# Spacing x's k-tiles 2176 instead of 2048 bytes apart in SBUF, in a one-core hybrid encoder layer

## The chip, the cores and the metric

The kernel runs on one core of one Trainium2 chip. The metric is the device time of one execution in microseconds (us). Three runs of the kernel before gave 1111.41, 1112.29 and 1112.52 us, so the time before is 1112.29 us.

The engines are named as in the profile: PE (TensorE, matmuls), PEld (TensorE loading the stationary operand), DVE (VectorE), ACT (ScalarE), POOL (GpSimd) and SP (which issues DMAs). SBUF is the on-chip memory with 128 partitions; an address below is the number of bytes from the start of a partition. PSUM is where matmuls accumulate.

## The reference

One encoder layer over 256 tokens of width 2048, all in float32:

```python
hn = _rmsnorm(h, norm_w[i])
proj = hn @ w_in[i]                       # 2048 -> 9 x 2048
q, v, f_fwd, f_bwd, z_a, b_gate, c_gate, h_b, z_b = jnp.split(proj, IN_SPLITS, axis=-1)
o_a = _hgrn2_bidirectional(jax.nn.silu(q), v, f_fwd, f_bwd, lb_all[:, i])
o_a = _head_rmsnorm(o_a, hgrn_norm_w[i]) * jax.nn.silu(z_a)
y_b = b_gate * _short_conv(c_gate * h_b, conv_w[i])
o_b = _rmsnorm(y_b, conv_norm_w[i]) * jax.nn.silu(z_b)
h = h + jnp.concatenate([o_a, o_b], axis=-1) @ w_out[i]      # 4096 -> 2048
gate = jax.nn.sigmoid(h @ w_ple_gate[i])                     # 2048 -> 2048
h = h + (p[i] @ w_ple[i]) * gate
return _rmsnorm(h, final_norm_w)
```

Most of the arithmetic is the product of x with w_in.

## The kernel before

**Splitting.** A float32 matrix is held as two parts, a rounded high part and the rest as a low part, and a product is made of three: high by high, high by low, low by high. Weights come from HBM in tiles of 1 MB into `raw` buffers (three of them in turn). ACT writes the high part into an `spl` buffer (L121), DVE the low part (L122). There are five `spl` buffers of 8192 bytes per partition, in turn. x is split once at the start into `xs` (L367 and L368), which stays until the last projection has ended.

**xs.** It has 16 k-tiles, one for each 128 rows of x transposed. A k-tile holds the high part (256 tokens, 1024 bytes) and behind it the low part (1024 bytes).

**The projections.** `gemm_part` makes, for each k-tile and each half m of 256 output columns, two matmuls: L427 with the weights' high part stationary and the whole k-tile (512 columns) moving, and L425 with the weights' low part stationary and x's high part alone (256 columns) moving. So a k-tile has two pairs of L427 and L425. There are 56 such projections: three at the start that advance together, and 53 of 16 k-tiles each. In some projections the order of the four matmuls is turned in k-tiles 1 and 3, or 9 and 11 (`TURNED`, `LATER`). The first value and gate projections (`gemm_two`, L446 to L448) and the later ones (`half` and `three`, L547 to L549) have x stationary and 512 columns of weights moving. All of these read xs. The output product (`pa`, `pb`), the gate (`pg<-spl,ht`) and the per-layer embedding (`pp<-spl,pt`), L547 to L549 and L1026 to L1028, do not.

**Order.** A scheduler sets each engine's order by priorities; only the first three projections are written out by hand. The weights are fetched ahead of their use through SP's queue.

**Small buffers.** `wz` is a block of zeros for 13 matmuls that run ahead of the first weights (L266). `early` is a buffer of 8192 bytes with the scans' mask in columns 0 to 255, later one of the norms (`rbc2`) in 256 to 511, the triangular masks in 512 to 1023, and two zeroed score buffers (`scm`) from 1024 and 1536; POOL fills it at the start (L277 to L290). `mx`, `et` and `esum` serve the lower bounds of the forget gates, once. `rw` holds the tokens' norms spread over 128 columns, for two matmuls once (L402).

**Places.** The allocator's addresses, in bytes, with the place modulo 1024:

| buffer | address | modulo 1024 |
|---|---|---|
| spl, five | 54208, and 8192 more each | 960 |
| xs, k-tile k | 95168 + 2048 k | 960 |
| ht0, after xs | 111552 | 960 |
| mixb, mixa (concatenated branches) | 147392, 196544 | 960 |
| pt (embedding input, split) | 172000 | 992 |
| s (scores, tag "s") | 187840 | 448 |
| early | 18304 | 896 |

Within an spl buffer the parts lie 1024 bytes apart, and the second half of 128 output columns 512 bytes behind the first. So a stationary operand begins at 960 or at 448 modulo 1024.

Of the kernel before, what the change touches and what calls it, by code (L numbers as in the profile page):

```python
# [8 lines left out]
F32 = mybir.dt.float32  # L9
F32R = mybir.dt.float32r  # L10
# [7 lines left out]
P = 128  # L18
D = 2048
T = 256  # L20
NKT = D // P
# [116 lines left out]
def tile_hymba_encoder(  # L138
# [15 lines left out]
    act, dve, pool, pe = nc.scalar, nc.vector, nc.gpsimd, nc.tensor  # L154
    out2 = out[0].rearrange("(m p) d -> p m d", p=P)

    const = ctx.enter_context(tc.tile_pool(name="const", bufs=1))
# [3 lines left out]
    xsp = xsctx.enter_context(tc.tile_pool(name="xsp", bufs=1))  # L161
# [3 lines left out]
    xp = xctx.enter_context(tc.tile_pool(name="xp", bufs=1, side="left"))  # L165
# [43 lines left out]
    for u in range(2):  # L209
        for half in range(2):  # L210
            oblocks.append([])
            for q in ORDER:
                k = 16 * half + 2 * q
# [21 lines left out]
    rx, rb, rf, most, dummy = (few[:, 2 * j : 2 * j + 2] for j in range(5))  # L235
# [21 lines left out]
    cvw, th = vec[:, 3:6, :], vec[:, 6:10, :].rearrange("p (d j) c -> p d j c", d=2)  # L257


    wz = const.tile([P, P], F32, name="wz")  # L260
    dve.memset(wz, 0.0)

    act.activation(dummy[:, 0:1], wz[:, 0:1], AF.Copy)
# [6 lines left out]
    ident = const.tile([P, P], F32, name="ident")  # L270
# [1 line left out]
    ones = const.tile([P, 1], F32, name="ones")  # L272
    pool.memset(ones, 1.0)

    early = const.tile([P, 2048], F32, name="early")
    smask = early[:, 0:T]
    pool.memset(smask, 1.0)  # L277
    pool.memset(smask.rearrange("p (c t) -> p c t", t=CH)[:, :, 0:1], 0.0)
# [16 lines left out]
        dve.memset(t, 0.0)  # L295


    mx = const.tile([P, 2, 16], F32, name="mx")
    et = const.tile([P, 2, 2, 16], F32, name="et")
    esum = const.tile([P, 2, 16], F32, name="esum")  # L300
    lb = const.tile([P, 2, 16], F32, name="lb")
    oml = const.tile([P, 2, 16], F32, name="oml")
    noml = const.tile([P, 2, 16], F32, name="noml")
# [57 lines left out]

    xs = xsp.tile([P, NKT, 2, T], F32R, name="xs")

    def x_split(kt):
        act.activation(xs[:, kt, 0, :], xf32[:, kt, :], AF.Copy, scale=nw[:, kt : kt + 1])  # L367
# [5 lines left out]
    rbc = const.tile([P, T], F32, name="rbc")  # L373
    rbc2 = early[:, T : 2 * T]
    ss8 = const.tile([P, 2, 4], F32, name="ss8")
    rw = [const.tile([P, P], F32, name=f"rw{m}") for m in range(2)]

    def load_tokens(m):
        nc.sync.dma_start(xf32[:, 8 * m : 8 * m + 8].rearrange("p k t -> p (k t)"), xtok[:, m])
# [12 lines left out]
    def x_norms():  # L392
        dve.tensor_reduce(out=rx, in_=ss8, op=ALU.add, axis=AX.X)
        act.activation(rx, rx, AF.Sqrt, bias=epst, scale=1.0 / D)
        dve.reciprocal(out=rx, in_=rx)
        for m in range(2):
            dve.tensor_copy(rw[m], rx[:, m : m + 1].broadcast_to([P, P]))

    def norms_spread():
        rps = psm.tile([P, 512], F32, tag="y", name="rps")  # L400
        for m in range(2):
            pe.matmul(rps[:, m * P : (m + 1) * P], lhsT=rw[m], rhs=ident, start=True, stop=True)  # L402
        dve.tensor_copy(rbc, rps[:, :T])  # L403
        dve.tensor_tensor(out=rbc2, in0=rbc, in1=rbc, op=ALU.mult)

# [114 lines left out]
    ap_ = actx.enter_context(tc.tile_pool(name="ap", bufs=1, side="right"))  # L520
    for m in range(2):
        at(2 + m, lambda m=m: load_tokens(m))
    for c in range(4):
        at(6 + c, lambda c=c: x_squares(c))
    at(11, x_norms)
    at(14, norms_spread)


# [395 lines left out]
    for i in range(8):  # L924
# [50 lines left out]
        for src, z, n in ((mixa, i - 1, len(SUMS)), (mixb, i - SUMS[0], len(sumb32))):  # L975
            if 0 <= z < n:
                k = 2 * SUMS[z]
# [3 lines left out]
                else:  # L981
                    t = ctmp.tile([P, 4, P], F32, tag="hb", name=f"sb{i}", bufs=2)
# [80 lines left out]
    for u in range(2):  # L1063
# [9 lines left out]
        for src, sums, main, other, scale in ((mixa, suma, psg, psm, False), (mixb, sumb, psm, psg, True)):  # L1073
            name = f"p{'ab'[scale]}{u}"
            acc = four(main, name)
            parts = oblocks[2 * u + scale]
            if u == 0 and not scale:
                for z in range(len(SUMS)):
                    k = 2 * SUMS[z]
# [186 lines left out]
```

## Time and profile before

| | |
|---|---|
| median of three runs | 1112.29 us (1111.41 to 1112.52) |
| the profiled execution | 1112.2 us, of which the span from first to last instruction is 1110.5 us |
| granted TensorE clock | 0.998 |
| PE busy | 1100.5 us, 99% |
| PEld busy | 945.7 us, 85% |
| DVE busy | 851.4 us, 77% |
| ACT busy | 677.3 us, 61% |
| POOL busy | 269.1 us, 24% |

A line of a group has the source line, the engine, the operation, output and inputs by the program's names, the shapes and the count; then the busy time in us and the mean duration of one in ns; then the engine's idle time ahead of them. Matmuls overlap, so their durations add up to more than the time that they take; a row of the timeline begins with the start in us, and the distance from one start to the next says how long a matmul holds the engine. A line of the form `L783 ... x16: 723/748/769, 90.8 to 501.3` has the least, median and greatest duration in ns, then the first and last start in us.

### The profile page before, as it was taken

To read this page: it belongs to the slowest core of one execution; us is meant where nothing else is said; L and a number is where in the kernel's file an instruction comes from. 1 tells how busy PE (TensorE), PEld (TensorE's weight loads), DVE (VectorE), ACT (ScalarE), POOL (GpSimd) and SP (SyncE) were. 2 spreads that over 40 slices of the span, in tenths; PEclk is the share of its full clock that TensorE was granted. 3 is DMA by queue.
4 is the path that set the end of the run, shared out by engine and by line. 5 is a ranking of instruction groups with operands and counts; after the bars stand their busy time and mean duration, and the time that the engine had idled before them with its cause. 6 is when DMAs were issued, how large, how long until landed. Compare 5 with 4: busy or idle time off the path is not lost.

```text
span 1110.5 us, 16882 instructions
## 1 busy us (share of the span) xinstructions
PE 1100.5 (99%) x6455; PEld 945.7 (85%) x6455; DVE 851.4 (77%) x1127; ACT 677.3 (61%) x946; POOL 269.1 (24%) x215
## 2 busy tenths in 40 slices
PE   9999999999999999999999999999999999999997
PEld 8888888888888888888888888888888888888886
DVE  7799578896889778997657758856667888887673
ACT  6786577667876697575545535535546575575562
POOL 1045015203530325043334223424331000000101
PEclk9999999999999999999999999999999999999999
DMA  9755454564457744758999998999979887887542
GB/s 340 272 187 190 153 190 157 171 242 153 161 162 258 292 152 152 231 172 228 298 310 250 270 334 231 282 345 254 288 196 306 318 299 286 286 312 253 193 133 76
DMA packets 69808, 260.44 MB, mean 235 GB/s; under 512 B 7008, under 2 KB 16608, under 8 KB 52192
## 3 DMA queue, kind: packets, MB, share of 16 engines
q1 hardware_dynamic: 60480, 242.25, 62.1%
q0 software_dynamic: 8960, 16.78, 10.0%
q8 instruction: 51, 0.84, 0.3%
q10 hardware_dynamic: 288, 0.34, 0.1%
q14 instruction: 29, 0.24, 0.1%
HBM read 257.25 MB, written 35.65 MB: 264 GB/s over the span
## 4 chain that ended last, share of the span: by engine, by line
PE 98%; DMA 1%; ACT 0%; SPq 0%; DVE 0%; DVEq 0%; issue 0%; ACTq 0%
PE a L427 37%; PE a L425 19%; PE avz L547 3%; PE avz L548 3%; PE avz L549 3%; PE pg L1027 3%; PE pg L1026 3%; PE pg L1028 3%; PE pa L547 2%; PE pa L548 2%; PE pa L549 2%; PE a L446 1%; PE a L448 1%; PE a L447 1%; PE pb_sc L548 1%; PE pb_sc L549 1%
## 5 line engine op out<-in xcount | busy, mean ns | idle before, releaser
L122 DVE TENSOR_TENSOR spl<-raw,spl 128x1024 fp32r<-128x1024 f32 (+2 forms) x419 | 505.0, 1219 | 163.6 <-ACT spl L121 160.2
L427 PE MATMUL a<-xs,spl 128*128 128x512 f32 x1792 | 617.3, 395 | 0.6 <-ACT spl L121 0.6
L121 ACT CAST spl<-raw 128x1024 fp32r<-128x1024 f32 (+2 forms) x419 | 414.1, 999 | 255.0 <-PE a L425 81.9
L425 PE MATMUL a<-xs,spl 128*128 128x256 f32 x1792 | 483.8, 278 | 0.0
L427 PEld LDWEIGHTS a<-xs,spl 128*128 128x128 f32 x1792 | 332.2, 188 | 73.6 <-ACT spl L121 1.0
L425 PEld LDWEIGHTS a<-xs,spl 128*128 128x128 f32 x1792 | 334.6, 188 | 5.8 <-DVE spl L122 0.5
L1143 POOL TENSOR_TENSOR hh<-hh,fw 128x512 f32<-128x512 f32 (+1 forms) x9 | 11.0, 1227 | 250.7 <-ACT gt L1142 248.0
L487 ACT COPY r<-a 128x256 f32<-128x256 f32 x112 | 40.5, 368 | 37.3 <-PE a L425 35.8
L547 PE MATMUL avz<-spl,xs 128*128 128x512 f32 x138 | 54.0, 391 | 0.0
L549 PE MATMUL avz<-spl,xs 128*128 128x512 f32 x138 | 53.7, 389 | 0.0
L548 PE MATMUL avz<-spl,xs 128*128 128x512 f32 x138 | 53.7, 389 | 0.0
L1026 PE MATMUL pg<-spl,ht 128*128 128x512 f32 (+1 forms) x120 | 45.2, 377 | 0.0
L1027 PE MATMUL pg<-spl,ht 128*128 128x512 f32 (+1 forms) x120 | 45.1, 376 | 0.0
L1028 PE MATMUL pg<-spl,ht 128*128 128x512 f32 (+1 forms) x120 | 45.0, 375 | 0.0
L716 POOL TENSOR_TENSOR qc<-pf,ge 128x256 f32<-128x256 f32 x16 | 18.3, 1148 | 105.8 <-ACT dd L706 91.8
L492 POOL TENSOR_TENSOR xf<-xf,rbc 128x1024 f32<-128x1024 f32 x8 | 19.9, 2486 | 94.0 <-DVE rbc L403 50.2
L121 ACT CAST spl<-early 128x1024 fp32r<-128x1024 f32 (+1 forms) x29 | 28.7, 990 | 19.1 <-PE pb_y L549 7.5
L122 DVE TENSOR_TENSOR spl<-early,spl 128x1024 fp32r<-128x1024 f32 (+1 forms) x29 | 32.9, 1147 | 9.2 <-ACT spl L121 8.8
L547 PE MATMUL pa<-spl,mixa 128*128 128x512 f32 x88 | 34.5, 392 | 0.0
L549 PE MATMUL pa<-spl,mixa 128*128 128x512 f32 x88 | 34.3, 389 | 0.0
L548 PE MATMUL pa<-spl,mixa 128*128 128x512 f32 x88 | 34.2, 389 | 0.0
L716 POOL TENSOR_TENSOR kc<-dd,ge 128x256 f32<-128x256 f32 x16 | 27.7, 1728 | 19.8 <-DVE dd L707 13.6
(321 smaller groups left out, 1641.7 us busy)
## 6 DMA issues: line engine op xcount, KB each, us to landing
raw<-in_w_in_dram SPq DMA_DIRECT2D x106, 1024.0 KB, 6.9
raw<-in_w_in_dram SPq DMA_DIRECT2D x100, 256.0 KB, 3.9
raw<-in_w_out_dram SPq DMA_DIRECT2D x36, 512.0 KB, 5.2
sums<-in_w_out_dram SPq DMA_DIRECT2D x32, 512.0 KB, 10.6
raw<-in_w_in_dram SPq DMA_DIRECT2D x26, 512.0 KB, 5.2
raw<-sums SPq DMA_DIRECT2D x13, 1024.0 KB, 5.3
raw<-in_w_gate_dram SPq DMA_DIRECT2D x9, 1024.0 KB, 5.1
sums<-in_w_out_dram POOLq DMA_DIRECT2D x16, 512.0 KB, 10.1
```

The source lines that it names most:

```text
L121: self.nc.scalar.copy(out=v[:, :, 0], in_=r)
L122: self.nc.vector.tensor_tensor(out=v[:, :, 1], in0=r, in1=v[:, :, 0], op=ALU.subtract)
L425: pe.matmul(a[:, :T], lhsT=lhsT, rhs=xs[:, kt, 0, :], start=False, stop=(kt == NKT - 1))
L427: pe.matmul(a, lhsT=lhsT, rhs=xs[:, kt, :, :].rearrange("p s n -> p (s n)"), start=(kt == 0), stop=False)
L487: act.copy(out=r, in_=acc[m][:, 1, :])
L547: pe.matmul(acc, lhsT=ah, rhs=w[:, 0], start=start, stop=False)
L548: pe.matmul(acc, lhsT=ah, rhs=w[:, 1], start=False, stop=False)
L549: pe.matmul(acc, lhsT=al, rhs=w[:, 0], start=False, stop=stop)
L716: pool.tensor_tensor(out=c64(dst[:, d]), in0=c64(src[:, d, :, half * P : (half + 1) * P]), in1=g.unsqueeze(3).broadcast_to([P, 2, 2, CH]), ...
L1026: pe.matmul(acc[m], lhsT=lh, rhs=wh, start=(kt == 0), stop=False)
L1027: pe.matmul(acc[m], lhsT=lh, rhs=wl, start=False, stop=False)
L1028: pe.matmul(acc[m], lhsT=ll, rhs=wh, start=False, stop=(kt == nk - 1))
```

## The change

A k-tile of xs gets 32 unused numbers (128 bytes) behind its 2048 bytes. xs grows by 2048 bytes per partition, from 32768 to 34816. To make room, four groups of constants lose their own places: wz (512 bytes) becomes columns 1024 to 1151 of early; mx, et and esum (512 bytes) go to the pool of x's first copy; the two rw (1024 bytes) become one tile that shares the buffer of tag "s".

```diff
-    wz = const.tile([P, P], F32, name="wz")
+    early = const.tile([P, 2048], F32, name="early")
+    wz = early[:, 1024 : 1024 + P]
...
-    early = const.tile([P, 2048], F32, name="early")
...
-    mx = const.tile([P, 2, 16], F32, name="mx")
-    et = const.tile([P, 2, 2, 16], F32, name="et")
-    esum = const.tile([P, 2, 16], F32, name="esum")
+    mx = xp.tile([P, 2, 16], F32, name="mx")
+    et = xp.tile([P, 2, 2, 16], F32, name="et")
+    esum = xp.tile([P, 2, 16], F32, name="esum")
...
-    xs = xsp.tile([P, NKT, 2, T], F32R, name="xs")
+    xs = xsp.tile([P, NKT, 2 * T + 32], F32R, name="xs")[:, :, : 2 * T].rearrange("p k (s t) -> p k s t", s=2)
...
-    rw = [const.tile([P, P], F32, name=f"rw{m}") for m in range(2)]
...
+        rw.append(ap_.tile([P, 2, P], F32, tag="s", name="rw"))
         for m in range(2):
-            dve.tensor_copy(rw[m], rx[:, m : m + 1].broadcast_to([P, P]))
+            dve.tensor_copy(rw[0][:, m], rx[:, m : m + 1].broadcast_to([P, P]))
+
+    rw = []
...
-            pe.matmul(rps[:, m * P : (m + 1) * P], lhsT=rw[m], rhs=ident, start=True, stop=True)
+            pe.matmul(rps[:, m * P : (m + 1) * P], lhsT=rw[0][:, m], rhs=ident, start=True, stop=True)
```

The addresses after: spl at 52160 and xs at 93120, both 2048 less and at 960 modulo 1024 as before, but k-tile k of xs now begins at 960 + 128 k modulo 1024. ht0 lies at 109504, 2048 less; mixa, mixb and pt stay. Early goes to 17216 (832 modulo 1024), s to 167168 (256), and the identity for transposes to 25440, 512 off its old place modulo 1024. All of these remain at the same place modulo 64.

Every engine has the same instructions in the same order as before. Two waits are added. One is on POOL, at the start of the program; before it has (names are buffers, `waits` names the engines whose semaphore is waited for):

```order
L277 MEMSET early 128x256
masks.py:199 ISA
masks.py:199 AFFINE_SELECT ident<-ident 128x128 [waits Pool_49]
L278 MEMSET early 128x4 [waits Pool_49]
L281 MEMSET early 128x512
L290 MEMSET early 128x512
L284 AFFINE_SELECT early<-early 128x128 [waits Pool_49]
L284 AFFINE_SELECT early<-early 128x128 x3
L290 MEMSET early 128x512
L292 MEMSET gx 128x20
```

and after:

```order
L277 MEMSET early 128x256
masks.py:199 ISA
masks.py:199 AFFINE_SELECT ident<-ident 128x128 [waits Pool_49]
L278 MEMSET early 128x4 [waits Pool_49]
L281 MEMSET early 128x512
L290 MEMSET early 128x512 [waits PE_49,Activation_49]
L284 AFFINE_SELECT early<-early 128x128 [waits Pool_49]
L284 AFFINE_SELECT early<-early 128x128 x3
L290 MEMSET early 128x512
L292 MEMSET gx 128x20
```

The first zeroing of scm (L290) now waits for the readers of wz, the 13 matmuls and one instruction of ACT, since wz is a part of the same columns. The other added wait is DVE's for its own earlier work, at the first sum of mixb into tmp ahead of the output product: tmp now begins 2048 bytes lower, over the places of hb.

## The prediction

> **What bounds the kernel now.** I read the page first: busy shares, the slices, the chain that ended last.
>
> ```profile
> span 1110.5 us, 16882 instructions
> PE 1100.5 (99%) x6455; PEld 945.7 (85%) x6455; DVE 851.4 (77%) x1127; ACT 677.3 (61%) x946; POOL 269.1 (24%) x215
> PE   9999999999999999999999999999999999999997
> PEclk9999999999999999999999999999999999999999
> PE 98%; DMA 1%; ACT 0%; SPq 0%; DVE 0%; DVEq 0%; issue 0%; ACTq 0%
> PE a L427 37%; PE a L425 19%; PE avz L547 3%; PE avz L548 3%; PE avz L549 3%; PE pg L1027 3%; PE pg L1026 3%; PE pg L1028 3%; PE pa L547 2%; PE pa L548 2%; PE pa L549 2%; PE a L446 1%; PE a L448 1%; PE a L447 1%; PE pb_sc L548 1%; PE pb_sc L549 1%
> ```
>
> TensorE is busy in every slice at full granted clock and makes 98% of the chain. No transfer and no other engine sets the time, so all that counts is how closely one matmul follows another. L427 and L425, whose moving operand is xs, hold 56% of the chain.
>
> Next, the groups by line and shape. They give the numbers of matmuls that touch xs: as moving operand (L427, 512 columns; L425, 256) and as stationary operand (L446 to L448, L547 to L549).
>
> ```profile
> L427 PE MATMUL a<-xs,spl 128*128 128x512 f32 x1792 | 617.3, 395 | 0.6 <-ACT spl L121 0.6
> L425 PE MATMUL a<-xs,spl 128*128 128x256 f32 x1792 | 483.8, 278 | 0.0
> L547 PE MATMUL avz<-spl,xs 128*128 128x512 f32 x138 | 54.0, 391 | 0.0
> L446 PE MATMUL a<-spl,xs 128*128 128x512 f32 x64 | 25.2, 394 | 0.0
> ```
>
> A matmul's 395 ns is not its price: matmuls overlap. The price is the distance between starts, so I read the timeline of TensorE, where the first column is the start in us. Over three projections in a row (first and last L427 of 96):
>
> ```profile
> 601.79 0.39 PE L427 MATMUL a<-xs,spl 128*128 128x512 f32 x1
> ...
> 634.73 0.40 PE L427 MATMUL a<-xs,spl 128*128 128x512 f32 x1
> ```
>
> 32.94 us over 95 steps is 346.7 ns for a pair of L427 and L425, with VectorE, ScalarE and DMAs at work all the while. The same code also runs in another rhythm, near the start (first and last L427 of 31):
>
> ```profile
> 13.98 0.40 PE L427 MATMUL a<-xs,spl 128*128 128x512 f32 x1
> ...
> 24.58 0.40 PE L427 MATMUL a<-xs,spl 128*128 128x512 f32 x1
> ```
>
> 10.60 us over 30 steps is 353.3 ns a pair, 6.6 ns more. The operands lie at the same places in SBUF as in the quick stretch (the weights' buffers repeat modulo 1024), so those places do not force either rhythm. The last view sets two groups of 512-column matmuls side by side: the gate's (stationary ht, at 960 or 448 modulo 1024) and the embedding's (stationary pt, 32 bytes further on). Both take their moving operand from spl.
>
> ```profile
> 1043.61 0.39 PE L1027 MATMUL pg<-spl,ht 128*128 128x512 f32 x1
> ...
> 1045.88 0.39 PE L1028 MATMUL pg<-spl,ht 128*128 128x512 f32 x1
> ...
> 1052.93 0.40 PE L1026 MATMUL pp<-spl,pt 128*128 128x512 f32 x1
> ...
> 1054.80 0.40 PE L1028 MATMUL pp<-spl,pt 128*128 128x512 f32 x1
> ```
>
> The gate's take 2.27 us over ten steps, 227.0 ns; the embedding's 1.87 us over eight, 233.8 ns. So a place in SBUF can cost a 512-column matmul 6.8 ns. All that the change does comes down to one question: is a step of 128 bytes such a place, or only one off a 64-byte line?
>
> **The change part by part.** Each engine's instructions keep their number, shape and order; no DMA is moved. What is left is places and two added waits.
>
> *The k-tiles of xs.* Before, every k-tile begins at 960 modulo 1024; after, k-tile k begins at 960 + 128k. Weights stay at 960 or 448. Modulo 512 the distance between what streams and what is loaded was always 0; now it is 0 for k = 0, 4, 8, 12 and not for the other 12 of 16. No row before has a distance of 128, 256 or 384 between operands of this kind, so the price is bounded from both sides by the 6.6 and 6.8 ns above, the one step in which matmul spacing differs here. Upper end: one step on each 512-column matmul in 12 of 16 k-tiles. That is 1792 x 3/4 = 1344 of L427, and (3 x 64 + 3 x 138) x 3/4 = 455 with xs stationary, the three lines of each group counted alike: 1799 x 6.8 ns = +12.2 us. Lower end: one step less on as many, -12.2 us; the two rhythms allow no reason to exclude a gain, since something periodic costs a step in one of them. I take 0. The nearest row is the embedding's: it is off by half a 64-byte line, while 128 bytes are two whole lines, and 960, 448 and 960 + 128k are all whole multiples of 64. A stream of 512 numbers then touches as many lines as before. Sixteen columns at the quick spacing of 227.0/512 ns each are 7.1 ns, about the step of 6.8: it looks like the price of one more line, and none is added. It is an inference from one pair of rows, so both ends stay.
>
> By the Trainium skill (TensorE: Matmul & The Clock Gate, Part 2, on loading weights) TensorE has two independent read ports, and loading the next weights takes nothing from the running matmul. By that rule alone the sum would also be +0, and neither end could happen. But the rule would give both groups above one spacing, and the trace has 227.0 and 233.8: the measurement decides, and the ends keep their chances.
>
> *The warm-up's zeros move into early.* The 13 warm-up matmuls now read what POOL sets to zero at L290, so that memset gains a wait for TensorE and ScalarE, and the rest of POOL's first queue stands behind it.
>
> ```profile
> 1.13 5.74 PE L266 MATMUL wps<-wz 128*128 128x128 f32 x26 [1.13 <-DVE wz L261]
> 2.10 0.52 POOL L290 MEMSET early<- 128x512 f32 x1
> 2.58 1.02 POOL L284 TENSOR_SCALAR_AFFINE_SELECT early<-early 128x128 f32<-128x128 f32 x4
> 4.01 0.11 POOL L292 MEMSET gx<- 128x20 f32 x1
> 54.29 2.40 POOL L492 TENSOR_TENSOR xf<-xf,rbc 128x1024 f32<-128x1024 f32 x1 [50.18 <-DVE rbc L403]
> L783 DVE COPY_PREDICATED early<-early,scps x16: 723/748/769, 90.8 to 501.3; 128x512 f32<-128x512 uint32 x16
> ```
>
> The memset starts at 6.9 instead of 2.1 us and POOL ends near 8.9 instead of 4.1. POOL has nothing to do until 54.29, and the masks are first used at 90.8: hidden, 0. If that cover were gone, it would cost 4.8 us. But the four selects, 1.02 us, now fall among VectorE's first splits:
>
> ```profile
> 6.72 0.42 DVE L122 TENSOR_TENSOR spl<-raw,spl 128x256 fp32r<-128x256 f32 x1
> 7.23 0.48 DVE L368 SCALAR_TENSOR_TENSOR xs<-xf,vec,xs 128x256 fp32r<-128x256 f32 x1
> 8.90 0.43 DVE L122 TENSOR_TENSOR spl<-raw,spl 128x256 fp32r<-128x256 f32 x1 [1.19 <-ACT spl L121]
> ```
>
> VectorE waits 1.19 us there for ScalarE, which is itself late, so a delay of some tenths is absorbed; between 0 and +1.0 us, I take 0. The Trainium skill (SBUF — State Buffer, Who interferes with whom) speaks against the change here: a VectorE instruction with two SBUF inputs and a GpSimd one that reads SBUF shut each other out for a whole instruction. By that rule, as an estimate with all four selects in the way, the sum would be +1.0 us; no row of before shows the two together at this place.
>
> *The rest.* The lower bounds' buffers go to xp, the two spread norms to the buffer of tag s. The order of use is unchanged, the spread norms are read long before s is first written, and 384 to 1024 bytes moved cost no instruction: 0. A VectorE instruction of the drain (tmp from mixb) gains a wait for VectorE's own earlier work, which stands ahead of it in the same queue: 0. The buffers that follow xs lie 2048 bytes lower, which changes which k-tile each covers; all k-tiles are read by the same last projection: 0.
>
> *The sum*: 0 + 0 + 0. It is made on the profiled execution: 1112.2 us with its span of 1110.5, and 1.7 us around it; the median of the three runs is 1112.29, so both agree within 0.1 us. Forecast 1112.3 us.
>
> **The rivals.**
>
> *Slower, by distance.* A distance other than 0 modulo 512 costs the step, whatever the lines. For it: the embedding's 233.8 ns is also a case of a distance that is not 0. Against it: that is the only such case, and it is off the 64-byte line too. Price +12.2 us, 1124.5 us, spread over 0 to 835 us in all projections. It decides from 330 matmuls on: 330 x 6.8 = 2.2 us.
>
> *Slower, by rhythm.* The turned orders of k-tiles 1 and 3 bring TensorE from the 353.3 into the 346.7 ns rhythm today. If a shifted x undoes this, 1792 pairs less some 40 that are slow already, by 6.6 ns: +11.6 us, 1123.9 us. For it: both rhythms hold on by themselves for many pairs. Against it: in the quick one nothing has to be avoided.
>
> *Faster.* What costs a matmul its step is the meeting of two reads at one place, and the shift takes it away in 12 of 16 k-tiles: 1344 pairs by 6.6 ns is -8.9 us, 1103.4; with the 455 others down to 1100.1. For it: the existence of two rhythms under one layout. Against it: the quoted groups of 512 columns last 391 to 395 ns each, so none stands out as quicker, and the one group at another distance is the slower.
>
> **How the numbers follow.** A difference of 0.2% (2.2 us) is about what can be told from no change in this kernel. No effect 0.44; slower by distance 0.19; slower by rhythm 0.12; faster 0.25. So faster 0.25, same 0.44, slower 0.31. The likeliest gives 1112.3, alone 1110.5 to 1114.0: the runs' spread of 1.1 us, and 1.0 for the start. The two signs hold over half the chance, so the range for 8 in 10 goes to both priced ends, 1100 to 1124.5, and leaves out mixtures beyond one step.
>
> **What would show it.** Right: L427 in the three projections after 602 us still 346.7 ns apart, the gate's matmuls 227; POOL's L290 near 6.9 us; VectorE's first splits at the same times. Slower by distance: k-tiles 0, 4, 8, 12 at 346.7 a pair and the others near 353, in every projection and in the value and gate products too. Slower by rhythm: all sixteen alike at 353. Faster: the others near 340. I am wrong if those twelve k-tiles differ from the four in either direction, or if the spacing changes by more than one step.

## The result and the profile after

| | before | after |
|---|---|---|
| median | 1111.90 us (4 runs, 1111.41 to 1112.52) | 1119.83 us (4 runs, 1119.20 to 1120.71) |
| ratio, 95% interval | | 1.0072 (1.0054 to 1.0089) |
| span of the profiled execution | 1110.5 us | 1117.8 us |
| granted clock | 0.998 | 0.997 |

The change costs 7.9 us. In the kernel after, L429 and L427 are the former L427 and L425, L448 to L450 the former L446 to L448, L549 to L551 the former L547 to L549. The page of after, with the span, the busy times and the chain that ended last:

```profile
span 1117.8 us, 16883 instructions
PE 1107.8 (99%) x6455; PEld 952.1 (85%) x6455; DVE 856.0 (77%) x1127; ACT 678.4 (61%) x946; POOL 263.1 (24%) x215
PE 97%; DMA 1%; DVE 1%; ACT 1%; SPq 0%; issue 0%; POOL 0%; DVEq 0%; ACTq 0%
```

TensorE has the same 6455 matmuls and is busy 7.3 us longer, which is the whole difference of the spans. It is still the chain, so the time went into the distance between matmuls. Groups by line and shape:

```profile
L429 PE MATMUL a<-xs,spl 128*128 128x512 f32 x1792 | 621.6, 394 | 0.4 <-ACT spl L121 0.4
L427 PE MATMUL a<-xs,spl 128*128 128x256 f32 x1792 | 491.1, 282 | 0.0
```

The long matmul's mean duration is 394 ns against 395 before, the short one's 282 against 278. Durations say little here. The starts say it: the timeline of TensorE over the same three projections (first and last L429 of 97).

```profile
605.70 0.39 PE L429 MATMUL a<-xs,spl 128*128 128x512 f32 x1
...
639.30 0.39 PE L429 MATMUL a<-xs,spl 128*128 128x512 f32 x1
```

33.60 us over 96 steps is 350.0 ns for a pair, against 346.7 before. By the trace's starts in ns (a printed row is rounded to 10), the k-tiles alternate: 703.3 ns for an even one, 696.7 for an odd one, where before every one took 693.3. No k-tile kept its old spacing.

With xs stationary the k-tiles differ. Two of them in the same product, the value and gate projections (first and last matmul of twelve, k-tile 10 and then k-tile 11):

```profile
461.46 0.39 PE L549 MATMUL avz<-spl,xs 128*128 128x512 f32 x1
...
463.95 0.40 PE L551 MATMUL avz<-spl,xs 128*128 128x512 f32 x1
464.19 0.40 PE L549 MATMUL avz<-spl,xs 128*128 128x512 f32 x1
...
466.75 0.40 PE L551 MATMUL avz<-spl,xs 128*128 128x512 f32 x1
```

K-tile 10 lies 10 x 128 = 1280 bytes further from the start of xs than before, a multiple of 256: 2.49 us over eleven steps, 226.4 ns. K-tile 11 lies 1408 bytes further, 128 more than a multiple of 256: 2.56 us, 232.7 ns. The place does cost, and 256 bytes off, which the prediction counted as off, is free here.

Where the 7.3 us went, by sums of start-to-start distances over all matmuls of a group:

| matmuls | before, us | after, us | difference |
|---|---|---|---|
| xs moving (1792 pairs) | 625.19 | 629.14 | +3.95 |
| xs stationary, 512 columns (633) | 144.54 | 147.08 | +2.54 |
| xsum stationary, in the same products (108) | 24.48 | 24.98 | +0.50 |
| mixa stationary, output product (288) | 65.63 | 66.34 | +0.71 |
| ht, mixb, suma, pt stationary | 163.97 | 163.95 | -0.02 |

The start of the program took 0.31 us less. Mixa's 0.71 us is mostly one wait, which the waits of after show:

```profile
PE pa L550 <- DVE spl L122: 0.4, 1, 0.4
```

At the start, the timeline of POOL, VectorE and TensorE:

```profile
6.68 0.53 POOL L290 MEMSET early<- 128x512 f32 x1 [4.52 <-PE wps L267]
7.16 1.20 POOL L284 TENSOR_SCALAR_AFFINE_SELECT early<-early 128x128 f32<-128x128 f32 x4
8.76 0.11 POOL L292 MEMSET gx<- 128x20 f32 x1
53.86 2.41 POOL L494 TENSOR_TENSOR xf<-xf,rbc 128x1024 f32<-128x1024 f32 x1 [44.98 <-DVE rbc L405]
6.99 0.48 DVE L368 SCALAR_TENSOR_TENSOR xs<-xf,vec,xs 128x256 fp32r<-128x256 f32 x1
8.29 0.43 DVE L122 TENSOR_TENSOR spl<-raw,spl 128x256 fp32r<-128x256 f32 x1 [0.82 <-ACT spl L121]
6.31 0.48 PE L429 MATMUL a<-xs,spl 128*128 128x512 f32 x1
```

POOL's zeroing waits for the warm-up and ends far ahead of its next task at 53.86; the first real matmul starts at 6.31 us (6.62 before).

### The profile page after: what moved, and what is told of

Same layout as the page of the kernel before. It is cut to its first block, busy times and chain, and to the rows that moved or that the text cites. A ratio compares the mean times of both kernels' runs of the same rounds, so it can differ in the third digit from the quotient of the medians.

```text
span 1117.8 us, 16883 instructions
## 1 busy us (share of the span) xinstructions
PE 1107.8 (99%) x6455; PEld 952.1 (85%) x6455; DVE 856.0 (77%) x1127; ACT 678.4 (61%) x946; POOL 263.1 (24%) x215
## 4 chain that ended last, share of the span: by engine, by line
PE 97%; DMA 1%; DVE 1%; ACT 1%; SPq 0%; issue 0%; POOL 0%; DVEq 0%; ACTq 0%
PE a L429 37%; PE a L427 19%; PE avz L549 3%; PE avz L551 3%; PE avz L550 3%; PE pg L1029 3%; PE pg L1028 3%; PE pg L1030 3%; PE pa L550 1%; PE pa L551 1%; PE a L448 1%; PE a L450 1%; PE pa L549 1%; PE a L449 1%; PE pb_sc L551 1%; PE pb_sc L550 1%
## 5 line engine op out<-in xcount | busy, mean ns | idle before, releaser
L429 PE MATMUL a<-xs,spl 128*128 128x512 f32 x1792 | 621.6, 394 | 0.4 <-ACT spl L121 0.4
L427 PE MATMUL a<-xs,spl 128*128 128x256 f32 x1792 | 491.1, 282 | 0.0
L429 PEld LDWEIGHTS a<-xs,spl 128*128 128x128 f32 x1792 | 332.4, 188 | 71.1 <-ACT spl L121 0.7
L427 PEld LDWEIGHTS a<-xs,spl 128*128 128x128 f32 x1792 | 336.9, 189 | 5.8 <-DVE spl L122 0.7
L549 PE MATMUL avz<-spl,xs 128*128 128x512 f32 x138 | 54.6, 396 | 0.0
L551 PE MATMUL avz<-spl,xs 128*128 128x512 f32 x138 | 54.3, 393 | 0.0
L549 PE MATMUL pa<-spl,mixa 128*128 128x512 f32 x88 | 34.5, 392 | 0.0
L551 PE MATMUL pa<-spl,mixa 128*128 128x512 f32 x88 | 34.3, 390 | 0.0
```

The source lines that it names most:

```text
L427: pe.matmul(a[:, :T], lhsT=lhsT, rhs=xs[:, kt, 0, :], start=False, stop=(kt == NKT - 1))
L429: pe.matmul(a, lhsT=lhsT, rhs=xs[:, kt, :, :].rearrange("p s n -> p (s n)"), start=(kt == 0), stop=False)
L549: pe.matmul(acc, lhsT=ah, rhs=w[:, 0], start=start, stop=False)
L551: pe.matmul(acc, lhsT=al, rhs=w[:, 0], start=False, stop=stop)
```

## The experiments

All but the last have the constants of the kernel after, keep xs's tile at 34816 bytes, and change where the k-tiles lie in it; all128 and all32 also shift the buffers ahead of it. Two operands are called level when their places are the same modulo 256. Theories: *lines* (only places off a 64-byte line cost; the loss comes from the constants or the waits), *distance* (what costs is the distance between the operand that streams and the one that is loaded), *alternation* (what costs is that this distance changes from k-tile to k-tile), *rhythm* (TensorE falls into a slower sequence by itself), and the absolute place of xs.

**x0: the pitch alone undone.**

```diff
-    xs = xsp.tile([P, NKT, 2 * T + 32], F32R, name="xs")[:, :, : 2 * T].rearrange("p k (s t) -> p k s t", s=2)
+    xs = xsp.tile([P, NKT * 2 * T + 512], F32R, name="xs")[:, 0 : 0 + NKT * 2 * T]
+    xs = xs.rearrange("p (k s t) -> p k s t", k=NKT, s=2)
```

> The k-tiles of xs are 2048 bytes apart again (the 2048 spare bytes lie behind xs), the constants stay where the change put them. All three theories (the distance between streamed and loaded operand modulo 256 counts; only its alternation from k-tile to k-tile counts; an operand's own place modulo 256 counts) expect the time of before, 1112 us within 1, with 346.7 ns a pair of the projection's matmuls and 227 ns for a 512-column matmul with xs stationary. If the moved constants or the added wait at the start cost something, it is 1113 to 1114, and the wait of 0.4 us at the start of the output product stays.

Measured: 1113.55 us, ratio 1.0011 (1.0000 to 1.0022). Most of the loss is the pitch. The constants and waits cost 0.2% at most, but they may not be free: 1113.55 us lies in the band of 1113 to 1114 that was named for that case, though the wait at the output product is gone, and x256 and step256 below, with the same constants and xs level, also have medians 1.4 to 1.5 us above the kernel before. Whether that is a cost of the constants stays open.

**x128 and x256: the old pitch, the whole of xs 128 or 256 bytes further on.** In the second line of x0's edit:

```diff
-[:, 0 : 0 + NKT * 2 * T]
+[:, 32 : 32 + NKT * 2 * T]     # x128; 64 instead of 32 in x256
```

> k-tiles 2048 bytes apart, but xs as a whole begins 128 bytes later, so every k-tile is 128 bytes off the weights modulo 256, none alternates. Distance theory: the 512-column matmuls with xs stationary take 231 to 234 ns instead of 227 in all k-tiles (633 x 4 to 7 ns, +2.5 to 4.4 us), the pairs with xs moving 350 to 353 ns (+6 to 12 us): 1120 to 1128 us. Place theory: the same numbers. Alternation theory: 346.7 and 227, 1112 us.

> As the last, but xs begins 256 bytes later. Distance and place theories, both modulo 256: as before, 1112 us, 346.7 ns a pair and 227 ns. If it is modulo 512 instead, the slow numbers of the shift by 128: 1120 to 1128 us. Alternation theory: 1112 us.

Measured: x128 1123.26 us, ratio 1.0096 (1.0078 to 1.0115); x256 1113.37 us, 1.0011 (1.0000 to 1.0021), as x0. The timeline of x128 (first and last L430, the long matmul there, of 96):

```profile
605.95 0.40 PE L430 MATMUL a<-xs,spl 128*128 128x512 f32 x1
...
639.30 0.40 PE L430 MATMUL a<-xs,spl 128*128 128x512 f32 x1
```

33.35 us over 95 steps is 351.1 ns a pair. A constant shift of 128 bytes costs more than the pitch of 2176, in which half the k-tiles lie 128 off; one of 256 bytes costs nothing beyond x0's time.

**all128: distance or absolute place.** x0 with an unused tile of 128 bytes ahead of all buffers on the left side. spl, xs, xsum and ht all move by 128 bytes together. mixa, mixb and suma, at the other end of SBUF, stay, and so are now 128 bytes off their weights.

```diff
+    const.tile([P, 32], F32, name="gap")
```

> k-tiles 2048 bytes apart, and 128 bytes of unused space ahead of all buffers on that side: the weights' buffers, xs, its sums, the transposed residual all move from 960 to 64 modulo 1024 together, while mixa, mixb and suma (stationary in the output product) stay at 960. Distance theory: projections and value products as before (346.7 a pair, 227), but the output product with mixa, mixb and suma stationary goes to 231 to 234 ns, some 600 matmuls x 4 to 7 ns: 1114.5 to 1116.5 us. Place theory: the projections slow too, 350 to 353 a pair, 1120 us or more. Alternation theory: 1112 us.

Measured: 1116.00 us, ratio 1.0029 (1.0016 to 1.0042). First the projections of all128 (first and last L431 of 97), then matmuls of the output product with mixb stationary (first and last of 31), then the same ones before (31):

```profile
602.75 0.39 PE L431 MATMUL a<-xs,spl 128*128 128x512 f32 x1
...
636.03 0.39 PE L431 MATMUL a<-xs,spl 128*128 128x512 f32 x1
```

```profile
876.85 0.40 PE L551 MATMUL pb_sc<-spl,mixb 128*128 128x512 f32 x1
...
883.83 0.39 PE L551 MATMUL pb_sc<-spl,mixb 128*128 128x512 f32 x1
```

```profile
877.02 0.39 PE L547 MATMUL pb_sc<-spl,mixb 128*128 128x512 f32 x1
...
883.82 0.39 PE L547 MATMUL pb_sc<-spl,mixb 128*128 128x512 f32 x1
```

The projections keep 33.28 us over 96 steps, 346.7 ns, though xs lies exactly where it lay in x128. The output product, whose own buffers were not touched, goes from 6.80 to 6.98 us over thirty steps, 226.7 to 232.7 ns. The cost moved to the products whose two operands had been parted. That is distance; absolute place falls.

**all32: the line theory's own test.** The same with 32 bytes of gap: spl, xs, xsum and ht begin half a 64-byte line off, as pt and held always did.

```diff
+    const.tile([P, 8], F32, name="gap")
```

> k-tiles 2048 bytes apart, 32 bytes of unused space ahead of the left side's buffers: the weights' buffers, xs, its sums and the transposed residual go from 960 to 992 modulo 1024, so all of them begin in the middle of a 64-byte line; pt and held, at 992, are then at distance 0 from them, while mixa, mixb and suma, at 960, are 32 off. Distance theory: projections and value products as before (346.7 ns a pair, 227 ns); the embedding's matmuls fall from 233.8 to 227 ns and the last gate block's from 233 to 227; the output product's with mixa, mixb, suma go to 233: 648 x 6.3 ns less 72 x 6.5 ns, +3.6 us, 1115 to 1116.5 us. Line theory (a start off a 64-byte line costs, as the prediction had it): everything reads one line more, projections 353 or more a pair and all 512-column matmuls 233 or more: 1125 us or more.

Measured: 1117.06 us, ratio 1.0039 (1.0023 to 1.0055). The projections (97 rows again) and the product with mixb (31 rows):

```profile
602.65 0.39 PE L431 MATMUL a<-xs,spl 128*128 128x512 f32 x1
...
635.93 0.39 PE L431 MATMUL a<-xs,spl 128*128 128x512 f32 x1
```

```profile
876.93 0.40 PE L551 MATMUL pb_sc<-spl,mixb 128*128 128x512 f32 x1
...
883.93 0.40 PE L551 MATMUL pb_sc<-spl,mixb 128*128 128x512 f32 x1
```

Both operands off a line together cost nothing (346.7 ns). mixb, on a line with its weights off, takes 233.3 ns; that the weights are off a line is not the reason, since xs stationary under the same weights keeps its spacing here (228.4 ns on average, 228.3 before). And in all128 both operands of mixb lie on whole lines, yet cost 232.7 ns. The line theory falls. pt, now level with its weights, goes from 234.0 to 230.0 ns on average. One expectation failed: held is level as well, and its 24 matmuls stay at 232.3 (232.9 before). They stand three in turn with three of 256 columns, and in the level pairs, which also mix 512 and 256 columns, a long matmul takes 230 to 233 ns by the trace's starts. So this may be the price of the mixed sequence; no run separates it.

**step256: varying places, all whole multiples of 256 off.** The 128 bytes of two neighbouring k-tiles stand together behind every second one, the rest as after (`Xs` only finds a k-tile in it).

```diff
-    xs = xsp.tile([P, NKT, 2 * T + 32], F32R, name="xs")[:, :, : 2 * T].rearrange("p k (s t) -> p k s t", s=2)
+    xs_all = xsp.tile([P, NKT // 2, 4 * T + 64], F32R, name="xs")
...
+            v = xs_all[:, first // 2, : 4 * T].rearrange("p (k s t) -> p k s t", k=2, s=2)
```

> As the kernel after, but the 32 unused numbers of two neighbouring k-tiles stand together behind every second one: 256 unused bytes after k-tiles 1, 3, 5 and so on. Same size of xs, same places of all other buffers, same constants; k-tile k begins at 960 + 256 x floor(k/2) modulo 1024, so that the distance to the weights changes from k-tile to k-tile as it does after, but is always 0 modulo 256. Distance modulo 256: pairs of L427 and L425 346.7 ns apart in all k-tiles, xs stationary 228 ns, 1112 to 1114 us, as with pitch 2048. If what costs is that the place of xs moves from k-tile to k-tile, or that a distance of 256 or 768 bytes differs from 0 and 512: about 350 ns a pair and 1118 to 1121 us.

Measured: 1113.75 us, ratio 1.0007 (0.9997 to 1.0016), with the gaps, the constants and the waits of after all in. What separates it from after is that no k-tile lies 128 off modulo 256. The stretch of the other kernels has 346.7 ns a pair here too. Its profiled execution, 1115.93 us, also shows what may lie behind the scatter of runs: a weight tile that landed late, and the slow rhythm after it. ACT's row, then three rows of TensorE, then its waits, then the rhythm in a later stretch (L438, first and last of 96):

```profile
666.38 1.05 ACT L121 CAST spl<-raw 128x1024 fp32r<-128x1024 f32 x1 [8.73 <-DMA raw<-in_w_in_dram]
```

```profile
668.54 0.39 PE L438 MATMUL a<-xs,spl 128*128 128x512 f32 x1
668.77 0.35 PE L436 MATMUL a<-xs,spl 128*128 128x256 f32 x1
669.17 0.47 PE L438 MATMUL a<-xs,spl 128*128 128x512 f32 x1
```

```profile
PE a L436 <- DVE spl L122: 1.4, 2, 1.2
```

```profile
704.93 0.40 PE L438 MATMUL a<-xs,spl 128*128 128x512 f32 x1
...
738.49 0.40 PE L438 MATMUL a<-xs,spl 128*128 128x512 f32 x1
```

After the late tile, the step behind the short matmul at 668.77 is 0.40 us instead of 0.12. From there on TensorE is in the slow rhythm, 33.56 us over 95 steps or 353.3 ns a pair, for some 80 us; the wait of 1.2 us, at 674.5 us, finds it there already. It is back at 346.7 behind k-tiles 1 and 3 of the projection at 750 us, whose matmuls have the turned order. The profiled execution of x0 has the same slow stretch, from about 682 to 748 us, and leaves it at the same two k-tiles. It was in it for 3 us before that too, from 673.4 us on, behind a step that was 0.05 us too long; at 682 us no step ahead of it is too long by over 0.01 us. So a late tile can bring TensorE into the slow rhythm, but it needs none.

**x64, x192 and pitch2064: is any distance better than 0?** xs 64 or 192 bytes further on (16 or 48 numbers in x128's edit); and a pitch of 2064 bytes, with which the k-tiles lie 16k bytes off:

```diff
-[:, 0 : 0 + NKT * 2 * T]
+[:, 0 : 0 + NKT * 516]     # the line behind it takes the first 512 of each 516 numbers
```

> k-tiles 2048 bytes apart, xs as a whole 64 bytes later. Distance theory, modulo 256: 64 is not 0, so as for 128: 231 to 234 ns with xs stationary, 350 to 353 ns a pair, 1120 to 1125 us. If the distance counts modulo 64 or 128 only together with something else, between that and 1112. Faster than 1112 only if some distance is better than 0.

> k-tiles 2048 bytes apart, xs as a whole 192 bytes later, that is 64 bytes ahead of the weights modulo 256. If the two directions are alike, the same numbers as for 64; if it matters which of the two reads is ahead, another spacing: between 340 and 353 ns a pair.

> k-tiles 2064 bytes apart, so k-tile k lies 16 k bytes off the weights: a map of the distance modulo 256 in one kernel, read from the 512-column matmuls with xs stationary, by k-tile. Distance theory: k-tile 0 at 227 ns and most others at 231 to 234 ns; unknown which others are free. Line theory: k-tiles 0, 4, 8, 12 (whole lines of 64) at 227, the rest at 233. Time between 1116 and 1125 us by either.

Measured: x64 1121.63 us, ratio 1.0075 (1.0057 to 1.0093); x192 1122.95 and pitch2064 1121.35 us, one run each. In pitch2064, by the trace's starts without the steps of over 300 ns at a product's ends, xs stationary takes 229.4, 229.4 and 228.9 ns at distances of 0, 16 and 240, and 230.3 to 234.3 ns at the others, 234.3 at 128. k-tile 0 begins a product and took 229.0 ns before as well; the other k-tiles took 226.7 to 227.3 before. Against its own k-tile, no distance was quicker than 0.

**ptalign: the embedding set level.** The kernel before, with 32 unused bytes behind held, so that pt and held begin at 960 modulo 1024.

```diff
         held = gp.tile([P, 4, 2048], F32R, name="held")
+        gp.tile([P, 8], F32, name="gap")
```

> The kernel before, with 32 unused bytes at the end of the last pool, so that pt and held begin at 960 instead of 992 modulo 1024, as the weights do. Distance modulo 256: the embedding's pp matmuls go from 233.8 to 227 ns apart, 48 x 6.8 ns = 0.33 us less in the whole kernel, 1111.9 us, too little for the time to show. held's matmuls (gate, last quarter) stay at 232 to 233 ns, as they did when both ht and held lay at 992. If the embedding's spacing has to do with something else (its short chains, PSUM banks): no change, 233.8 ns.

Measured: 1111.75 us, ratio 1.0000 (0.9990 to 1.0011). Twelve of the embedding's matmuls (first and last):

```profile
1051.12 0.39 PE L1026 MATMUL pp<-spl,pt 128*128 128x512 f32 x1
...
1053.61 0.39 PE L1028 MATMUL pp<-spl,pt 128*128 128x512 f32 x1
```

2.49 us over eleven steps, 226.4 ns: the 233.8 that the prediction leant on is gone. Over all 48 it is 11.23 to 11.03 us. This is the only improvement that the runs pointed to, and it is too small to be seen in the time; no version beats the kernel before.

Mean distances in ns from a matmul's start to the next one's, over each whole kernel, without steps of over 400 ns (512 columns; a pair is 512 and 256). Off is how far xs lies from level with its weights, modulo 256:

| kernel | off | pair | xs stationary | mixa | mixb | pt |
|---|---|---|---|---|---|---|
| before | 0 | 348.3 | 228.3 | 227.9 | 226.7 | 234.0 |
| x0 | 0 | 349.2 | 228.5 | 228.4 | 226.7 | 234.1 |
| x256 | 0 | 348.4 | 228.5 | 228.3 | 226.7 | 234.4 |
| step256 | 0 | 349.5 | 228.5 | 227.8 | 226.7 | 234.4 |
| all128 | 0 | 348.3 | 228.6 | 233.5 | 232.8 | 234.5 |
| all32 | 0 | 348.1 | 228.4 | 234.2 | 233.2 | 230.0 |
| after | 0, 128 in turn | 350.7 | 232.4 | 228.5 | 226.7 | 234.3 |
| x64 | 64 | 351.1 | 234.7 | 228.4 | 226.7 | 234.0 |
| x128 | 128 | 352.3 | 234.0 | 227.8 | 226.7 | 233.9 |
| x192 | 192 | 353.7 | 230.4 | 228.0 | 226.7 | 234.3 |

x0's and step256's pairs hold the slow stretch described above. Those of x64 are a mixture: most of its projections run at 349 to 350 ns a pair, some at 353.

## Why the prediction was right or wrong

**The time** lay within the range, but the range ran from one priced end to the other, 24.5 us, and that it held says little. The forecast itself, no effect and 1112.3 us, was wrong by 7.5 us, on the side of a rival that had a chance of 0.19.

**The k-tiles: the step that failed.** "I take 0", by way of 64-byte lines, measured +7.0 us over the three groups that read xs or follow it. The row was the right one; the reading of it was wrong. pt differed from the gate's ht in two things at once, its place modulo 64 and its distance to the weights. all32 and all128 part them: off a multiple of 64 but level costs nothing (346.7 ns a pair in all32), on multiples of 64 but not level costs 6.0 ns (mixb in all128, 232.7 against 226.7). No run shows lines of 64 bytes at all; the 7.1 ns for "one more line" that met the step of 6.8 was a coincidence. pt was also not the only such case: held lies 32 bytes off its ht, at 232.9 ns, but in a mixed sequence that could not decide it.

**Slower, by distance: the right mechanism, with the wrong period and the wrong size.** The period: 256, not 512, since x256, step256 and k-tile 10 of after keep the old spacing. So 8 of 16 k-tiles are off, not 12. The stationary term, 455 x 6.8 = 3.1 us, came out at 2.54 + 0.50 = 3.04 us, but that is luck, since the numbers behind it differ: 330 matmuls are off and not 455, while some in level k-tiles and those of xsum, which follow at once, pay too. The moving term, 1344 x 6.8 = 9.1 us, came out at 3.95 us. Its signature failed: k-tiles 0, 4, 8 and 12 did not stay at 346.7 ns a pair. In the quoted stretch a pair costs 3.3 ns more on average (3.95 us over 1792 pairs is 2.2 ns), and it is the level k-tiles that are further apart, 703.3 against 696.7 ns. A delay that is carried on to the next matmul would do that, and xsum, level and behind an off xs, at 231.3 instead of 226.7 ns, fits it; no view shows the carrying itself. Even with all k-tiles 128 off, x128's pair takes 351.1 in the quoted stretch and not 353. I had one step for all of these, from matmuls of 512 columns behind each other, and no row of the mixed sequence.

By the Trainium skill (TensorE: Matmul & The Clock Gate, Part 2, on loading weights) loading takes nothing from the running matmul, and by that rule none of this could cost. The 226.7 and 232.7 ns of mixb, with the same places but for the weights', disagree.

**Slower, by rhythm.** Not the cause: after holds 350.0, not 353. But the rival's observation was real, that the slow rhythm holds on by itself for many pairs: step256 runs in it for 80 us behind one late tile. And the turned orders do what that rival said of them: in step256 and x0 the slow rhythm ends at k-tiles 1 and 3 of a projection with the turned order, in the kernel before at k-tiles 9 and 11 near 26 us.

**Faster** is refuted for the distances tried: 16 to 240 bytes, none quicker than 0. Its lowest end is also 0.2 us off: 8.9 and 455 x 6.8 ns leave 1100.3 us, not 1100.1.

**The warm-up's zeros** went as worked out: L290 at 6.68 us (6.9 forecast), POOL done at 8.87 (8.9), covered until 53.86, cost 0. The selects took 1.20 instead of 1.02 us, and VectorE's instructions 0.43 and 0.48 as before, since it stood idle from 7.47 to 8.29 us, for ScalarE. So the exclusion of the two engines that the Trainium skill states (SBUF — State Buffer, Who interferes with whom) had little to act on, and its +1.0 us did not come.

**The rest, 0.** The 0.4 us wait at the output product was not foreseen, but it follows neither the pitch nor the constants: it is 0.8 us in x256 and 0.3 in ptalign, which has the old constants and the old layout of xs, and there is none in x0 and x128. What the moved constants cost is not settled to better than 0.2% (x0).

## What to carry to other kernels

Where TensorE is the bound, lay the streamed and the loaded operand of neighbouring matmuls at the same place modulo 256 bytes: parting them cost up to some 3% of a 512-column matmul in float32r here, while moving both together cost nothing. A padding that seems harmless to every other engine can undo such an alignment, and only starts, not durations, show it. Before a price is read from two groups, list everything in which they differ.

## What the hardware showed beyond that

- The cost depends on direction: xs 64 bytes ahead gives 234.7 ns with xs stationary, 192 ahead (64 behind) 230.4. The pairs are 351.1 and 353.7, but there the rhythms mix in. Each is one profiled execution. In pitch2064, distances of 16 bytes either way cost over 2 ns against the same k-tile before (229.4 against 227.0, 228.9 against 226.7).
- It costs already when only the next matmul's stationary operand is off. In all32, sumb moves with its weights and stays level; by the trace's starts a sumb matmul takes 226.7 ns ahead of another one, but 235.0 (mean of 16) ahead of one with mixb stationary, which lies 32 bytes off.
- In a product of one shape the delay comes in a sequence rather than evenly: in x128's value and gate products the steps run 233, 241, 232, 231, 232, 228, 230 ns, and much the same again.
- TensorE has at least two stable rhythms for one and the same sequence of pairs, 346.7 and 353.3 ns. In step256 a weight tile landed late (ACT's split of it starts at 666.38 instead of 662.46 us), and the slow rhythm began with the first matmul that came late, by 0.28 us. In x0 it set in once behind a matmul that was 0.05 us late and once with none late at all. In both it ended for good in a projection with the turned order, some 80 and 66 us later.
- What in the hardware meets at a distance that isn't a multiple of 256 stays open: the runs vary addresses alone, and no view of the profile shows reads of SBUF.
